# A decoder layer's feed-forward weights: block sums of 20 column tiles formed early and kept in DRAM, and another place for the last gate

## The chip, the cores and the metric

One core of a Trainium2 chip runs the kernel as one launch. The metric is the device time of an execution in microseconds (us). Engines are named as the profiler names them: PE (TensorE, matmuls), PEld (its weight loads), DVE (VectorE), ACT (ScalarE), POOL (GpSimd), SP (SyncE, which here only issues DMA transfers). A matmul's outputs go to PSUM banks; everything else lies in SBUF, in numbered slots of a tag ("three raw slots" are three buffers that tiles take in turn), or in DRAM.

## The reference

One layer of a decoder, sequence 1024, width 1024, feed-forward width 2816, all in float32:

```python
h = rms_norm(x, norm1)
z = h @ w_in                       # pool channels | q | k | v | u_s | v_s | three gates of 1024
y_a = pool_mixer(x_pool, w_pool, pool_scale) @ w_proj_a
q, k = rope(rms_norm(q)), rope(rms_norm(k))
y_b = sliding_window_attention(q, k, v, sinks) @ w_proj_b
y_c = spatial_gating(u_s, v_s, w_s, b_s, sgu_v_norm) @ w_proj_c
merged = sigmoid(g0) * y_a + sigmoid(g1) * y_b + sigmoid(g2) * y_c
x = x + merged @ w_out
h = rms_norm(x, norm2)
up = causal_dwconv(h @ w_up, conv_w, conv_b)      # width 3, over 5632 channels
gate, val = split(up, 2)
x = x + (silu(gate) * val) @ w_down
```

## The kernel before

**Arithmetic.** PE takes operands in a reduced format, so each float32 operand is split into a hi part (ACT, L86, a rounding copy) and a lo part (DVE, L87, the difference), and each product is three matmuls: hi by hi, hi by lo, lo by hi. The raw tile, loaded by SP into one of three `raw` slots, is free again when both halves of its split are done. hi and lo parts go to `w` slots (four) or, in the up stage, to `q` slots (thirteen).

**The front** (L644 to L768) works for two halves t of 512 tokens. `tok_major` forms k, v, q, u and v of the gating; then come 26 units, each a column tile of 128 of w_in: `w_gran` loads 512 KB (L276) and splits it, one unit ahead of its matmuls (L173 to L175), and `proj_ac` or `proj_b` (L625) load the matching projection. Pooling, gating and attention are generators that are spawned with a due time and stepped by `tick` when `clock`, a count of PE's microseconds, reaches it. Attention's steps are DVE's L452 to L462, then PE's flips L469. A unit adds into `part`, a tile of one slot (16 KB in each partition, which is 2 MB). When all units of a half are done, the out projection runs (w_out by L247), while, for t = 1, `norm2_flip` normalises the rows of the first half, which have lain in four `x2` slots since t = 0. The slots `x2` thus stand empty until the last unit of t = 0 fills them, and `part` is not in use in the out projection of t = 0.

**The up stage** (L776 to L960) is h @ w_up by a scheme of seven products P1 to P7 in place of eight over halves of the tokens and of the contraction. Column tile c (of 22) holds g, the gate columns (`up_raw(0, c)`), and v, the value columns (`up_raw(1, c)`), each 512 KB (L599). With a11, a12 the upper and lower halves of g and a21, a22 those of v, four sums are formed by POOL, each of 128x512: s1 = a21 + a22 (L858), s2 = s1 - a11 (L859), s3 = a11 - a21 (L860), s4 = a12 - s2 (L861). They and a11, a12, a22 are split and multiplied with ready operands of the tokens (L898 to L900, twelve matmuls a product). For tiles 0 to 6 the products P1 and P2 (PRE) run first, while the second half of the tokens is being normalised; the other five (REST) run later, between those of tiles 7 to 21 (FULL). The order of products is the list `turns`. `up_prep` of a tile begins, with its loads, LOADS = 9 turns ahead of its product and must have split it READY = 7 turns ahead. `up` then adds the PSUM result to others on ACT (L904, L910) and DVE (L916, L919, L926, L928, L939). When a tile's last product is done, `gate` gets its two results: `conv` (ACT L871, twice DVE L875) for v and g, silu on ACT (L883), the product on DVE (L884), and SP's store of 512 KB to DRAM, `gd[c]` (L885). One step of the first gate in the list follows each product. The results lie in `x` slots (four).

**The down stage** (L981 to L1163) multiplies gd with w_down by a like scheme, in two parts of 6 and 5 pairs of tiles, seven products each; `todo` lists its 77 steps of twelve matmuls (L1143 to L1145 are the three of a product). `operands` splits each step's operand three steps ahead, hi into `w`, lo into the same `x` slots. The last gate's steps are stepped here, one at each of the first eight: `if j < 8: next(gates[-1], None)`. The second part's loads are issued by `fetch` at the first step of P4 of the first part.

**What sets the order.** SP, POOL, PE and, up to the down stage, DVE and ACT get their rows from a scheduler that orders the instructions by a simulated timeline; in the down stage DVE and ACT keep the order in which the code is written.

Of the kernel before, what the change touches and what calls it, by code (L numbers as in the profile page):

```python
# [6 lines left out]
F32 = mybir.dt.float32  # L7
# [6 lines left out]
P = 128  # L14
S = 1024
# [19 lines left out]
PRE_SETS = ((0, 1), (2, 3), (4, 5, 6))  # L35
LOADS, READY = 9, 7


def trunk_kernel(tc, x, positions, norm1, w_in, q_norm, k_norm, sinks, w_pool, pool_scale,
# [104 lines left out]
    tasks = []  # L144

    def tick():
# [126 lines left out]
    def w_gran(w, c0):  # L273

        rw = raw([P, KD, P])
        sp.dma_start(rw, w[:, c0 : c0 + P].rearrange("(k p) c -> p k c", p=P))  # L276
        hi = slot("w", 4, [P, KD, P], F32R)
# [324 lines left out]
    def up_split(src, wt):  # L602
        split(wt[:, 0], wt[:, 1], src)
        return wt

    def up_early(c):
        g = up_raw(0, c)
# [31 lines left out]
    h2d = [dp.tile([P, 2, T], F32, name=f"h2d{k}") for k in range(4)]  # L639
    gd = [dp.tile([P, S], F32, name=f"gd{c}") for c in range(NC_FF)]  # L640
    mark = [None]
    spawn(setup_rest(), 24)
    st = Stream(w_in, 768, 256, KD, normed.ins)
    for t in range(2):  # L644
# [100 lines left out]
        while tasks:  # L745
            step(tasks[0])
        ss = slot("ssx", 2, [P, 32], F32)[:, 0:8]
        if t == 0:
            h = new_h()
# [87 lines left out]
    def up_prep(c, names):  # L837


        ws = wss[c, names]  # L840
        g = up_raw(0, c)
        if names == PRE:
# [4 lines left out]
            return  # L847
        v = up_raw(1, c)
        if names == REST:
# [3 lines left out]
            sp.dma_start(st["ug"][:, 0:T], pre_d[c][:, 1, :])  # L853
        a11, a12, a21, a22 = g[:, 0:HK, :], g[:, HK:, :], v[:, 0:HK, :], v[:, HK:, :]
        sa, sb = q_([P, 2, HK, P]), q_([P, 2, HK, P])
        s1, s2, s3, s4 = sa[:, 0], sa[:, 1], sb[:, 0], sb[:, 1]
        yield
        pool.tensor_tensor(s1, a21, a22, ALU.add)  # L858
        pool.tensor_tensor(s2, s1, a11, ALU.subtract)  # L859
        pool.tensor_tensor(s3, a11, a21, ALU.subtract)  # L860
        pool.tensor_tensor(s4, a12, s2, ALU.subtract)  # L861
        for n in names:
            wt = slot("w", 4, [P, 2, HK, P], F32R) if n in ("P1", "P6", "P2") else q_([P, 2, HK, P], F32R)
            ws[n] = up_split({"P1": a11, "P2": a12, "P3": s4, "P4": a22, "P5": s1, "P6": s2, "P7": s3}[n], wt)
            yield

    def conv(u, c):
# [10 lines left out]
    def gate(c, ug, uv):  # L878
        for yv in conv(uv, NC_FF + c):
            yield  # L880
        for yg in conv(ug, c):
            yield
        act.activation(yg, yg, AF.Silu)  # L883
        dve.tensor_tensor(yg, yg, yv, ALU.mult)  # L884
        sp.dma_start(gd[c], yg)  # L885
# [228 lines left out]
    for j, (part, p, q) in enumerate(todo):  # L1114
# [100 lines left out]
```

## Time and profile before

| what | value |
|---|---|
| median of 3 runs | 1316.62 us (1316.19 to 1318.61) |
| the profiled execution | 1317.56 us |
| its span in the trace | 1315.9 us, granted TensorE clock .998 of full speed |
| PE busy | 98% of the span |
| DVE, ACT, POOL busy | 74%, 46%, 14% |
| moved by DMA | 151.25 MB, 115 GB/s over the span |

The span is the time from the first to the last recorded instruction. The shares are averages over stages: the front runs to about 653 us, the up stage to about 1089 us, the down stage to the end. Which engine PE waits for differs from stage to stage and is read from the waits of each.

### The profile page before, as it was taken

Reading aid. Unit: us, or ns where it says so; the run is one execution under the profiler, and the core shown is the slowest. Engines: PE = TensorE matmul, PEld = TensorE weight load, DVE = VectorE, ACT = ScalarE, POOL = GpSimd, SP = SyncE. Lnnn points to the kernel's source line nnn. Section 1 sums busy time; section 2 is a strip of 40 time slices with the busy share of each in tenths; the row PEclk is TensorE's granted clock in tenths of the full one; section 3 lists DMA queues with packets and bytes.
Section 4 is the critical chain, followed back from the end, with each engine's and each line's share of the span. In section 5 each row is a group of like instructions: output and inputs, shape, how many; then the busy total and the mean of one; then the engine's idle time right before and its main releaser. Section 6 shows DMA issues by size and latency. Waiting matters only on the chain.

```text
span 1315.9 us, 16097 instructions
## 1 busy us (share of the span) xinstructions
PE 1283.4 (98%) x5956; PEld 1062.3 (81%) x5956; DVE 969.5 (74%) x1516; ACT 605.3 (46%) x986; POOL 190.2 (14%) x123
## 2 busy tenths in 40 slices
PE   6999999999999999999998999999999999999998
PEld 6888888888888888888877878878788787788886
DVE  6786875644578776455494889899898885986986
ACT  5555554434465555233573444434444444443432
POOL 0000000000000000000004444344542420101202
PEclk9999999999999999999999999999999999999999
DMA  6322224422432222533455223333233309418615
GB/s 235 115 85 71 80 81 126 123 72 96 161 111 74 73 78 82 158 106 104 161 207 160 86 91 113 98 108 99 65 112 112 96 32 341 107 66 287 109 20 96
DMA packets 167645, 151.25 MB, mean 115 GB/s; under 512 B 7616, under 2 KB 132494, under 8 KB 167566
## 3 DMA queue, kind: packets, MB, share of 16 engines
q1 hardware_dynamic: 163533, 142.87, 34.1%
q0 software_dynamic: 4032, 7.34, 3.8%
q8 instruction: 47, 0.77, 0.2%
q14 instruction: 33, 0.26, 0.1%
HBM read 120.30 MB, written 29.88 MB: 114 GB/s over the span
## 4 chain that ended last, share of the span: by engine, by line
PE 62%; DVE 19%; DMA 8%; ACT 5%; issue 5%; POOL 1%; SPq 0%; DVEq 0%; ACTq 0%; POOLq 0%
PE mm L173 14%; PE mm L174 14%; PE mm L175 14%; DVE x L875 7%; DMA raw<-in_w_up_dram 4%; PE bk L1144 4%; PE bk L1145 4%; PE bk L1143 4%; DVE q L87 4%; ACT x L871 2%; DMA hq<-gd 2%; DVE w L87 2%; ACT w L86 1%; PE at L445 1%; ACT x L883 1%
## 5 line engine op out<-in xcount | busy, mean ns | idle before, releaser
L173 PE MATMUL mm<-hh,w 128*128 128x512 f32 x416 | 162.6, 391 | 0.0
L175 PE MATMUL mm<-hh,w 128*128 128x512 f32 x416 | 162.5, 391 | 0.0
L174 PE MATMUL mm<-hh,w 128*128 128x512 f32 x416 | 162.4, 390 | 0.0
L858 POOL TENSOR_TENSOR q<-raw 128x512 f32<-128x512 f32 x22 | 37.1, 1685 | 844.5 <-DMA sm<-pre 652.5
L87 DVE TENSOR_TENSOR w<-raw,w 128x1024 fp32r<-128x1024 f32 (+1 forms) x96 | 93.3, 976 | 88.4 <-ACT w L86 88.4
L86 ACT ACTIVATE w<-raw 128x1024 fp32r<-128x1024 f32 (+1 forms) x96 | 82.2, 857 | 155.3 <-PE mm L174 67.0
L875 DVE SCALAR_TENSOR_TENSOR x<-q,cA,x 128x1023 f32<-128x1023 f32 x88 | 135.2, 1541 | 19.6 <-ACT x L871 19.0
L898 PE MATMUL bk<-hq,q 128*128 128x512 f32 x352 | 139.2, 395 | 6.0 <-DVE sm L916 5.1
L899 PE MATMUL bk<-hq,q 128*128 128x512 f32 x352 | 137.7, 391 | 0.0
L900 PE MATMUL bk<-hq,q 128*128 128x512 f32 x352 | 137.4, 391 | 0.0
L1144 PE MATMUL bk<-x,w 128*128 128x512 f32 x308 | 120.2, 390 | 3.0 <-DVE x L87 3.0
L1145 PE MATMUL bk<-w,x 128*128 128x512 f32 x308 | 119.9, 389 | 0.0
L1143 PE MATMUL bk<-w 128*128 128x512 f32 x308 | 94.8, 390 | 1.8 <-ACT hq L1066 1.0
L174 PEld LDWEIGHTS mm<-hh,w 128*128 128x128 f32 x416 | 78.1, 188 | 16.2
L175 PEld LDWEIGHTS mm<-hh,w 128*128 128x128 f32 x416 | 78.1, 188 | 16.0
L173 PEld LDWEIGHTS mm<-hh,w 128*128 128x128 f32 x416 | 78.1, 188 | 15.7
L87 DVE TENSOR_TENSOR wa<-raw,wa 128x512 fp32r<-128x512 f32 x72 | 49.5, 695 | 54.6 <-ACT wa L86 54.6
L898 PEld LDWEIGHTS bk<-hq,q 128*128 128x128 f32 x352 | 66.3, 188 | 25.1 <-DVE sm L916 7.6
L871 ACT ACTIVATE x<-q,cA 128x1024 f32<-128x1024 f32 x44 | 54.0, 1241 | 69.6 <-DVE q L926 36.8
L86 ACT ACTIVATE wa<-raw 128x512 fp32r<-128x512 f32 x72 | 45.1, 631 | 78.4 <-PE mm L175 67.3
L900 PEld LDWEIGHTS bk<-hq,q 128*128 128x128 f32 x352 | 66.5, 189 | 14.1
L899 PEld LDWEIGHTS bk<-hq,q 128*128 128x128 f32 x352 | 66.5, 189 | 13.4
(267 smaller groups left out, 2947.0 us busy)
## 6 DMA issues: line engine op xcount, KB each, us to landing
raw<-in_w_in_dram SPq DMA_DIRECT2D x72, 512.0 KB, 3.9
raw<-in_w_up_dram SPq DMA_DIRECT2D x51, 512.0 KB, 4.9
gd<-x SPq DMA_DIRECT2D x22, 512.0 KB, 2.8
x<-in_x_dram SPq DMA_DIRECT2D x16, 512.0 KB, 4.3
raw<-in_w_out_dram SPq DMA_DIRECT2D x16, 512.0 KB, 3.6
hq<-gd SPq DMA_DIRECT2D x28, 256.0 KB, 5.3
hq<-in_w_down_dram SPq DMA_DIRECT2D x28, 256.0 KB, 5.3
raw<-in_w_proj_b_dram SPq DMA_DIRECT2D x32, 128.0 KB, 2.8
```

The source lines that it names most:

```text
L86: split.last = act.activation(hi, src, AF.Copy).ins
L87: dve.tensor_tensor(lo, src, f(hi), ALU.subtract)
L173: pe.matmul(ps, a(0), b(0), start=first, stop=False)
L174: pe.matmul(ps, a(0), b(1), start=False, stop=False)
L175: r = pe.matmul(ps, a(1), b(0), start=False, stop=last)
L875: dve.scalar_tensor_tensor(y[:, n:], u[:, 0 : S - n], col(w), y[:, n:], ALU.mult, ALU.add)
L898: pe.matmul(ps, ws[n][:, 0, k, :], rhs[n](0, k), start=start and k == 0, stop=False, skip_group_check=True)
L899: pe.matmul(ps, ws[n][:, 0, k, :], rhs[n](1, k), start=False, stop=False, skip_group_check=True)
L900: pe.matmul(ps, ws[n][:, 1, k, :], rhs[n](0, k), start=False, stop=k == HK - 1, skip_group_check=True)
L1143: pe.matmul(ps[i], hi[:, 0, ts], hi[:, 1, :], start=start, stop=False, skip_group_check=True)
L1144: pe.matmul(ps[i], hi[:, 0, ts], lo[:, 1, :], start=False, stop=False, skip_group_check=True)
L1145: pe.matmul(ps[i], lo[:, 0, ts], hi[:, 1, :], start=False, stop=q == b - 1, skip_group_check=True)
```

## The change

The sums s1 to s4 of 20 of the 22 tiles (SUM_SETS; tiles 16 and 20 are left as they were) are formed in the front by a generator, `weight_sums`, that is stepped from `tick` like the other tasks: SP loads a tile's g and v into two scratch tiles, POOL forms the four sums in place, and POOL itself issues two stores of 512 KB to a new DRAM array, `ws`. There are three stretches: tiles 0 to 5 in the units of t = 0 from the 15th, in `x2` slots; tiles 6 to 11 in the out projection of t = 0 and the first units of t = 1, in the slot of `part`, which is allocated later for that; the last eight in the units of t = 1 from the 12th, again in `x2` slots. Since the rows of the first half then no longer stay in `x2`, they are read back from `out`, four loads of 512 KB, before the second norm. In the up stage such a tile loads only a22 of v and, for REST, nothing of g; SP loads the two pairs of sums from `ws` into `q` slots where POOL formed them before. These slots are taken READY turns ahead in place of LOADS. The last gate's two results move from `x` slots to raw slots, its steps to the down steps in GATE_STEPS, and it has one step more, ahead of the product.

```diff
+GATE_STEPS = (0, 2, 4, 12, 13, 14, 15, 16)
+SUM_SETS = (range(0, 6), range(6, 12), (12, 13, 14, 15, 17, 18, 19, 21))
+SUM_GAPS = (8.2, 8.2, 8.2)
...
     def tick():
+        while side_line and side_line[0][0] <= clock[0]:
+            side_step()
...
+    def weight_sums(cs, tiles, gap):
+        def take(c):
+            vg = tiles()
+            for o, dst in zip((1, 0), vg):
+                c0 = o * D_FF + c * P
+                with tc.issue_after(last_raw[0].ins):
+                    sp.dma_start(dst, w_up[:, c0 : c0 + P].rearrange("(k p) c -> p k c", p=P))
+            return vg
+        nxt = take(cs[0])
+        yield gap
+        for j, c in enumerate(cs):
+            v, g = nxt
+            a11, a12, a21, a22 = g[:, 0:HK], g[:, HK:], v[:, 0:HK], v[:, HK:]
+            pool.tensor_tensor(a22, a21, a22, ALU.add)
+            pool.tensor_tensor(a21, a11, a21, ALU.subtract)
+            pool.dma_start(s_d[c][:, 1], v)
+            pool.tensor_tensor(a11, a22, a11, ALU.subtract)
+            pool.tensor_tensor(a12, a12, a11, ALU.subtract)
+            pool.dma_start(s_d[c][:, 0], g)
+            yield gap / 2
+            if j + 1 < len(cs):
+                nxt = take(cs[j + 1])
+                yield gap / 2
...
-        part = slot("part", 1, [P, KD, T], F32)
...
         for i, c0 in enumerate(units):
+            if i == (14 if t == 0 else 11):
+                side_work(SUM_SETS[2 * t], own_tiles, SUM_GAPS[2 * t])
+            if i == 2:
+                side_end()
+                part = slot("part", 1, [P, KD, T], F32)
...
+                side_end()
                 x2t = [slot("x2" if t == 0 else "x", 4, [P, D], F32) for _ in range(NT)]
...
         if t == 0:
+            side_work(SUM_SETS[1], part_tiles(), SUM_GAPS[1])
+        else:
+            for b in range(NT):
+                x2[0][b] = slot("x2", 4, [P, D], F32)
+                sp.dma_start(x2[0][b], out[b * P : (b + 1) * P, :])
...
-        v = up_raw(1, c)
+        early = any(c in cs for cs in SUM_SETS)
+        if early:
+            v = raw([P, HK, P])
+            c0 = D_FF + c * P
+            sp.dma_start(v, w_up[T:, c0 : c0 + P].rearrange("(k p) c -> p k c", p=P))
...
         sa, sb = q_([P, 2, HK, P]), q_([P, 2, HK, P])
-        pool.tensor_tensor(s1, a21, a22, ALU.add)
-        pool.tensor_tensor(s2, s1, a11, ALU.subtract)
-        pool.tensor_tensor(s3, a11, a21, ALU.subtract)
-        pool.tensor_tensor(s4, a12, s2, ALU.subtract)
+        if early:
+            sp.dma_start(sa, s_d[c][:, 0].rearrange("p (j k) c -> p j k c", j=2))
+            sp.dma_start(sb, s_d[c][:, 1].rearrange("p (j k) c -> p j k c", j=2))
+        else:
...
     def conv(u, c, last):
-        y = slot("x", 4, [P, S], F32)
+        y = raw([P, S]) if last else slot("x", 4, [P, S], F32)
...
         act.activation(yg, yg, AF.Silu)
+        if last:
+            yield
         dve.tensor_tensor(yg, yg, yv, ALU.mult)
...
-        if j < 8:
+        if j in GATE_STEPS:
             next(gates[-1], None)
```

Line numbers in rows of the changed kernel are its own: L636, L637, L639, L640 are its four sums in the front, L638 and L641 their stores, L613 `up_raw`, L926 the load of a22, L938 and L939 the loads of sums, L975 the gd store, L962 and L974 conv and product of the gate, L90 the split's lo part.

POOL, before: its row of the mask, L342, in the front's start, and what stands behind it, the sums of the first tiles of the up stage in `q` slots.

```order
L342 AFFINE_SELECT sm_103_711<-sm_103_711 128x512
L858 TENSOR_TENSOR q_5989<-raw_5987 128x512
L860 TENSOR_TENSOR q_5990<-raw_5985,raw_5987 128x512
L859 TENSOR_TENSOR q_5989<-q_5989,raw_5985 128x512
L861 TENSOR_TENSOR q_5990<-raw_5985,q_5989 128x512
```

POOL in the changed kernel, from the same mask on: the first tile of the first stretch (x_296 and x_297 are its v and g in `x2` slots, ws_256 is tile 0 of `ws`).

```order
L356 AFFINE_SELECT sm_103_733<-sm_103_733 128x512
L636 TENSOR_TENSOR x_296_1972<-x_296_1972 128x512
L637 TENSOR_TENSOR x_296_1972<-x_297_1973,x_296_1972 128x512
L638 DMA ws_256<-x_296_1972 128x1024
L639 TENSOR_TENSOR x_297_1973<-x_296_1972,x_297_1973 128x512
L640 TENSOR_TENSOR x_297_1973<-x_297_1973 128x512
L641 DMA ws_256<-x_297_1973 128x1024
```

Each of 20 tiles now puts six rows there, before any row of the up stage; of the 88 sums of the up stage eight are left.

SP in the up stage, before: raw loads of g and v, what a REST tile reads back (`pre`), and a gate's store in between.

```order
L885 DMA gd_251<-x_8540 128x1024
L599 DMA raw_8450<-in_w_up_dram 128x8x128
L852 DMA sm_1317_8452<-pre_5769 128x512
L853 DMA q_8453<-pre_5769 128x512
L885 DMA gd_239<-x_8673 128x1024
L599 DMA raw_8512<-in_w_up_dram 128x8x128
L599 DMA raw_8514<-in_w_up_dram 128x8x128
```

SP in the changed kernel, at a like place (ws_259 are tile 3's sums, for REST, ws_270 those of tile 14).

```order
L975 DMA gd_245<-x_7434 128x1024
L613 DMA raw_7535<-in_w_up_dram 128x8x128
L933 DMA sm_1168_7475<-pre_5985 128x512
L934 DMA q_7476<-pre_5985 128x512
L938 DMA q_7539<-ws_259 128x1024
L939 DMA q_7540<-ws_259 128x1024
L975 DMA gd_236<-x_7579 128x1024
L926 DMA raw_7537<-in_w_up_dram 128x4x128
L938 DMA q_7599<-ws_270 128x1024
L939 DMA q_7600<-ws_270 128x1024
```

Two rows a tile, which wait for `q` slots, came into SP's queue, ahead of the gate's stores and of later raw loads.

DVE at the start of the down stage, before: splits of operands (L87), the last gate's conv (L875) in `x` slots, and sums of the down stage's own (L1020, L1021).

```order
L87 TENSOR_TENSOR x_9099<-hq_9023,w_9098 128x1024
L875 SCALAR_TENSOR_TENSOR x_9084<-q_8952,cA,x_9084 128x1023
L87 TENSOR_TENSOR x_9116<-hq_9026,w_9115 128x1024
L875 SCALAR_TENSOR_TENSOR x_9084<-q_8952,cA,x_9084 128x1022
L87 TENSOR_TENSOR x_9133<-hh_9007,w_9132 128x1024
L87 TENSOR_TENSOR x_9151<-hh_9012,w_9150 128x1024
L875 SCALAR_TENSOR_TENSOR x_9136<-q_8920,cA,x_9136 128x1023
```

DVE in the changed kernel, at the same place.

```order
L90 TENSOR_TENSOR x_9264<-hq_9188,w_9263 128x1024
L90 TENSOR_TENSOR x_9280<-hq_9191,w_9279 128x1024
L962 SCALAR_TENSOR_TENSOR raw_9249<-q_9117,cA,raw_9249 128x1023
L90 TENSOR_TENSOR x_9297<-hh_9172,w_9296 128x1024
L90 TENSOR_TENSOR x_9313<-hh_9177,w_9312 128x1024
L962 SCALAR_TENSOR_TENSOR raw_9249<-q_9117,cA,raw_9249 128x1022
L1110 TENSOR_TENSOR q_9317<-hh_9172 128x1024
```

The conv of the last gate's v stands two splits apart and in a raw slot; the conv of its g, which followed at once, comes some 20 rows later.

## Rows read from the trace of the kernel before

**Rows 1.** Page, part 1: busy us (share of the span) xinstructions.

```profile
PE 1283.4 (98%) x5956; PEld 1062.3 (81%) x5956; DVE 969.5 (74%) x1516; ACT 605.3 (46%) x986; POOL 190.2 (14%) x123
```

**Rows 2.** Stretches: us, busy of PE, PEld, DVE, ACT, POOL, PE clock, DMA share, GB/s.

```profile
693.00:726.00 33.00, 29.86 (x125) 24.16 (x125) 14.60 (x19) 11.83 (x22) 16.62 (x12) 0.95 0.53 157
726.00:1089.00 363.00, 357.62 (x1562) 291.85 (x1560) 322.36 (x334) 154.97 (x216) 146.64 (x77) 1.00 0.29 93
1188.00:1254.00 66.00, 66.00 (x293) 54.66 (x292) 48.59 (x48) 30.33 (x34) 14.12 (x16) 1.00 0.77 185
```

**Rows 3.** PE's waits, whole run: us in total, times, longest us.

```profile
PE bk L898 <- DVE sm L916: 5.1, 6, 1.5
PE bk L898 <- ACT w L86: 4.0, 2, 3.1
PE bk L1144 <- DVE x L87: 3.0, 3, 1.7
PE mm L173 <- DVE hh L91: 0.6, 1, 0.6
```

**Rows 4.** Timeline about 705: start us, us, what [idle before <-releaser].

```profile
700.15 1.29 POOL L858 TENSOR_TENSOR q<-raw 128x512 f32<-128x512 f32 x1 [652.45 <-DMA sm<-pre]
...
702.72 1.15 ACT L86 ACTIVATE q<-q 128x512 fp32r<-128x512 f32 x2 [3.37 <-POOL q L860]
...
705.44 0.50 PE L898 MATMUL bk<-hq,w 128*128 128x512 f32 x1 [3.14 <-ACT w L86]
```

**Rows 5.** Timeline about 768.

```profile
766.18 1.72 DVE L875 SCALAR_TENSOR_TENSOR x<-q,cA,x 128x1022 f32<-128x1022 f32 x1
...
768.55 0.50 PE L898 MATMUL bk<-hq,q 128*128 128x512 f32 x1 [1.15 <-DVE sm L916]
```

**Rows 6.** DVE groups while POOL is idle (1090 to 1130; 440 to 580): busy, mean ns | idle.

```profile
L875 DVE SCALAR_TENSOR_TENSOR x<-q,cA,x 128x1022 f32<-128x1022 f32 x2 | 2.6, 1278 | 0.0
...
L87 DVE TENSOR_TENSOR wp<-raw,wp 128x512 fp32r<-128x512 f32 x11 | 7.5, 686 | 0.1
```

**Rows 7.** DVE groups from 700 to 1060.

```profile
L875 DVE SCALAR_TENSOR_TENSOR x<-q,cA,x 128x1022 f32<-128x1022 f32 x38 | 64.8, 1706 | 0.4
L87 DVE TENSOR_TENSOR q<-q,q 128x512 fp32r<-128x512 f32 x62 | 63.7, 1036 | 11.0 <-ACT q L86 11.0
L875 DVE SCALAR_TENSOR_TENSOR x<-q,cA,x 128x1023 f32<-128x1023 f32 x38 | 55.5, 1459 | 17.1 <-ACT x L871 16.9
L87 DVE TENSOR_TENSOR q<-raw,q 128x512 fp32r<-128x512 f32 x21 | 26.4, 1258 | 0.0
...
L916 DVE TENSOR_TENSOR sm<-sm,bk 128x512 f32<-128x512 f32 x20 | 13.5, 676 | 0.0
```

**Rows 8.** DMA: issues (KB, us to landing); stretch 1089 to 1122; SP and ACT, 540 to 553.

```profile
raw<-in_w_up_dram SPq DMA_DIRECT2D x51, 512.0 KB, 4.9
...
out_dram<-sm POOLq DMA_DIRECT2D x16, 256.0 KB, 5.1
...
1089.00:1122.00 33.00, 30.88 (x134) 24.92 (x135) 21.61 (x20) 15.20 (x17) 0.00 (x0) 1.00 1.02 366
...
540.83 0.38 SPq L276 DMA_DIRECT2D raw<-in_w_in_dram  x1
...
552.09 1.06 ACT L86 ACTIVATE w<-raw 128x1024 fp32r<-128x1024 f32 x1 [4.58 <-PE mm L174]
```

**Rows 9.** POOL, whole run: one of its waits, and the group of L858.

```profile
POOL q L858 <- DVE x L875: 80.2, 7, 12.9
...
L858 POOL TENSOR_TENSOR q<-raw 128x512 f32<-128x512 f32 x22 | 37.1, 1685 | 844.5 <-DMA sm<-pre 652.5 <-DVE x L875 80.2 <-PE bk L900 65.7
```

**Rows 10.** Timeline of DVE at the start of the down stage.

```profile
1118.54 1.23 DVE L87 TENSOR_TENSOR x<-hq,w 128x1024 fp32r<-128x1024 f32 x1 [1.91 <-PE bk L1145]
```

**Rows 11.** Timeline of one attention block in the front, DVE and PE.

```profile
474.89 1.14 DVE L462 TENSOR_SCALAR t<-t,st 128x256 f32<-128x256 f32 x4
...
479.94 1.02 PEld L469 LDWEIGHTS at<-cA,t 128*128 128x128 f32 x8
```

More of the change, by code (lines that the diff above doesn't have):

```diff
@@ L144, in trunk_kernel, with side_step @@
     tasks = []
+    side_line = []
+    def side_step():
+        try:
+            side_line[0][0] = clock[0] + next(side_line[0][1])
+        except StopIteration:
+            side_line.pop(0)
     def tick():
+        while side_line and side_line[0][0] <= clock[0]:
+            side_step()
         again = True
@@ L275, in w_gran @@
         rw = raw([P, KD, P])
-        sp.dma_start(rw, w[:, c0 : c0 + P].rearrange("(k p) c -> p k c", p=P))
+        last_raw[0] = sp.dma_start(rw, w[:, c0 : c0 + P].rearrange("(k p) c -> p k c", p=P))
         hi = slot("w", 4, [P, KD, P], F32R)
@@ L604, in up_split, with own_tiles, part_tiles, tiles @@
         return wt
+    def weight_sums(cs, tiles, gap):
[21 more added lines that the diff above has]
+                yield gap / 2
+    def own_tiles():
+        return [slot("x2", 4, [P, KD, P], F32) for _ in range(2)]
+    def part_tiles():
+        big = slot("part", 1, [P, 4, KD, P], F32)
+        turn = [0]
+        def tiles():
+            turn[0] ^= 2
+            return big[:, turn[0]], big[:, turn[0] + 1]
+        return tiles
+    def side_work(cs, tiles, gap):
+        side_line.append([clock[0], weight_sums(cs, tiles, gap)])
+    def side_end():
+        while side_line:
+            side_step()
     def up_early(c):
@@ L640, in trunk_kernel @@
     gd = [dp.tile([P, S], F32, name=f"gd{c}") for c in range(NC_FF)]
+    s_d = [dp.tile([P, 2, KD, P], F32, name=f"ws{c}") for c in range(NC_FF)]
     mark = [None]
@@ L840, in up_prep @@
         ws = wss[c, names]
-        g = up_raw(0, c)
+        if names != REST:
+            g = up_raw(0, c)
         if names == PRE:
@@ L847, in up_prep @@
             return
-        v = up_raw(1, c)
+        early = any(c in cs for cs in SUM_SETS)
[4 more added lines that the diff above has]
+        else:
+            w2 = up_raw(1, c)
+            a21, v = w2[:, 0:HK, :], w2[:, HK:, :]
         if names == REST:
@@ L853, in up_prep, with conv @@
             sp.dma_start(st["ug"][:, 0:T], pre_d[c][:, 1, :])
-        a11, a12, a21, a22 = g[:, 0:HK, :], g[:, HK:, :], v[:, 0:HK, :], v[:, HK:, :]
+        yield
         sa, sb = q_([P, 2, HK, P]), q_([P, 2, HK, P])
-        s1, s2, s3, s4 = sa[:, 0], sa[:, 1], sb[:, 0], sb[:, 1]
-        yield
-        pool.tensor_tensor(s1, a21, a22, ALU.add)
-        pool.tensor_tensor(s2, s1, a11, ALU.subtract)
-        pool.tensor_tensor(s3, a11, a21, ALU.subtract)
-        pool.tensor_tensor(s4, a12, s2, ALU.subtract)
+        if early:
+            sp.dma_start(sa, s_d[c][:, 0].rearrange("p (j k) c -> p j k c", j=2))
+            sp.dma_start(sb, s_d[c][:, 1].rearrange("p (j k) c -> p j k c", j=2))
+        else:
+            a11, a12 = g[:, 0:HK, :], g[:, HK:, :]
+            pool.tensor_tensor(sb[:, 1], a21, v, ALU.add)
+            pool.tensor_tensor(sa[:, 0], sb[:, 1], a11, ALU.subtract)
+            pool.tensor_tensor(sb[:, 0], a11, a21, ALU.subtract)
+            pool.tensor_tensor(sa[:, 1], a12, sa[:, 0], ALU.subtract)
+        ab = {"P3": sa[:, 1], "P4": v, "P5": sb[:, 1], "P6": sa[:, 0], "P7": sb[:, 0]}
+        if names == FULL:
+            ab["P1"], ab["P2"] = g[:, 0:HK, :], g[:, HK:, :]
         for n in names:
             wt = slot("w", 4, [P, 2, HK, P], F32R) if n in ("P1", "P6", "P2") else q_([P, 2, HK, P], F32R)
-            ws[n] = up_split({"P1": a11, "P2": a12, "P3": s4, "P4": a22, "P5": s1, "P6": s2, "P7": s3}[n], wt)
+            ws[n] = up_split(ab[n], wt)
             yield
-    def conv(u, c):
+    def conv(u, c, last):
         col = lambda w: cvc[:, w * 44 + c : w * 44 + c + 1]
-        y = slot("x", 4, [P, S], F32)
+        y = raw([P, S]) if last else slot("x", 4, [P, S], F32)
         act.activation(y, u, AF.Identity, bias=col(3), scale=col(2))
@@ L878, in gate @@
     def gate(c, ug, uv):
-        for yv in conv(uv, NC_FF + c):
+        last = c + 1 == NC_FF
+        for yv in conv(uv, NC_FF + c, last):
             yield
-        for yg in conv(ug, c):
+        for yg in conv(ug, c, last):
             yield
         act.activation(yg, yg, AF.Silu)
+        if last:
+            yield
         dve.tensor_tensor(yg, yg, yv, ALU.mult)
```

1 line of the change is left out of this document (added).

## The prediction

> **What bounds the kernel now.** I read the busy times first, then busy time by stretch, then the waits of TensorE, then the rows around the longest of them. PE is busy for 1283.4 of 1315.9 us [rows 1]: nothing that adds matmuls can pay and nothing that removes other engines' work pays unless PE waits for it there. To see what PE loses I take its pitch from a stretch without a wait: 293 records begin or end in 66 us, two of them cut by the ends, so 291 matmuls of 512 columns fill it and one costs 66/291 = 0.2268 us [rows 2]. The same sum over the up stage gives two losses. From 693 to 726 us there are 123 whole matmuls, worth 27.9 us, in 33: 5.1 us are lost (A). From 726 to 1089 us there are 1560, worth 353.8, in 363: 9.2 us are lost (B) [rows 2]. The waits say where: L898 of `up` waits twice, 4.0 us, for ACT's split L86, and six times, 5.1 us, for DVE's L916; at the start of the down stage L1144 waits three times, 3.0 us, for DVE's split L87 (C). In the front PE waits for a DVE split but once, 0.6 us, after its start [rows 3]. So what can be had is A + B + C, and the front has nothing to give: it can only lose.
>
> **Whose fault A is.** PE stands 3.14 us at 705.44 for ACT's split of a hi part. ACT stood itself for 3.37 us until 702.72, for POOL's L860, and POOL had begun L858 only at 700.15 [rows 4]. The first sums of the stage come late, and PE pays. The granted clock, .95 over these 33 us [rows 2], costs 33 x .05 = 1.65 us of the 5.1.
>
> **Whose fault B is.** Ahead of the wait at 768.55, for L916, DVE runs the conv's L875 for 1.72 us from 766.18 [rows 5]. That L875 takes 1.28 us where POOL is idle [rows 6]. From 700 to 1060 us, where POOL works, the L875 of 1022 columns takes 1.706 in 38 cases, that of 1023 columns 1.459 in 38; a 512-column split of sums takes 1.036 in 62, and of raw data into the q slots 1.258 in 21 [rows 7]; the clean split of 512 takes 0.686 [rows 6]. The extra is 38 x .428 + 38 x .181 + 62 x .350 + 21 x .572 = 16.3 + 6.9 + 21.7 + 12.0 = 57 us of DVE over 88 POOL operations, .65 us each. DVE is busy 322 of the 363 us in B [rows 2], so such lumps reach PE.
>
> **The change part by part.** *Eighty POOL operations leave the up stage* (20 tiles by four). DVE gets 80 x .65 = 52 us of the 57 back there. A: P6's split then waits for a load of two sums, and no longer for four operations behind a load. The least is nothing, if the load is as late as the sums were; the most is 5.1. I take 4.5, since the load stands in SP's row as early as the raw one and lands without POOL's 2.6 us from 700.15 to 702.72. B: between nothing and 9.2. Two of 22 tiles keep their sums on POOL, and DVE's row order around L916 (L926, L875, L928, L875, L916) stays, so I let two of the six waits stand: 9.2 x 4/6 = 6.
>
> *Loads in the up stage.* A tile with ready sums reads 1 MB of sums and 256 KB less of v; a REST tile reads no g, 512 KB less. SP issues the sums seven turns ahead (READY) where the raw tiles are asked for nine ahead (LOADS). Seven turns are 7 x 12 x .2268 = 19.1 us, less 4.9 for the landing of 512 KB [rows 8]: about 14 us of cover. What stood at the slots before was POOL, at most 12.9 us at a time [rows 9], with nothing behind it but other sums. Now SP stands there, and the next raw loads and the gd store of `gate` stand behind it. I cost it at nothing because 12.9 is under 14; without that cover it is the second rival.
>
> *The last gate.* Its two results lie in raw slots, and its steps are spread to step 16 of the down stage. Before, DVE stood 1.91 us at 1118.54 for a slot of the operands' low parts [rows 10], two of whose four the gate held. C is the three waits' 3.0 [rows 3]. Most: all of it. Least: below nothing by one conv operation, 1.28 us [rows 6], if a split falls behind it at a new place. I take 2.5: two conv operations still stand between the first splits, and half a microsecond may stay. The last mult and its gd store come later too, at step 16 in place of 8. The loads that want that tile are the second part's `fetch`, at P4's first step, the 31st (five products by six pairs before it): 14 steps of 12 matmuls by .2268 are 38 us of cover for a store of 512 KB, where a load of that size lands in 4.9 [rows 8].
>
> *The front takes it all on.* POOL does 80 sums and 40 stores in three stretches; it has nothing else to do there, as its single idle time of 652.5 us shows [rows 9]. DVE pays the same 52 us there. By the longest row I have: at 474.89 DVE's L462 ends at 476.03 and the flips L469 that need it begin at 479.94, so attention has 3.9 us [rows 11], and four sums by .65 take 2.6. Loads and stores add 2.1 MB a tile, 42 MB in all, one tile in each gap of 8.2 us; a unit's own loads, 512 KB by `w_gran` and 512 KB by `proj_b`, come to 1.05. The 3.15 MB want 384 GB/s, and the most I see is 366 [rows 8]: a slip of .4 us a unit, 3 us over eight units. The tile asked for at 540.83 lands 3.9 us later and is split at 552.09, when PE frees the slot [rows 8]: 7 us of cover. SP waits there for slots too: a tile holds two of the four x2 slots for its landing, 4.9 [rows 8], its four operations, 6.7 by L858's 1.685 [rows 9], and its store, 5.1 for half the size through POOL's queue [rows 8]: 16.7 us and, for the other half, up to 5 more; the same slots are wanted again after two gaps, 16.4 us. So SP may stand some 3 us, at most 5, in `weight_sums`, with the raw loads of `proj_b` and `w_gran` behind it, under the same 7 us of cover. The reload of four residual tiles is 2 MB, 5.7 us at 366 GB/s, for the second norm, which runs beside the out projection's 192 matmuls, 43.5 us. Least loss nothing; most 8 us, if both slips, 3 and 5, came through uncovered. The nearest row is the front's own wait of .6 [rows 3]: I take two or three such, 1.5.
>
> The sum: 4.5 + 6 + 2.5 − 1.5 = 11.5 us. The profiled execution took 1317.56, so 1306.1; it lies .94 above the median of the runs, so **1305.1 us** against 1316.62. A difference under 0.2%, 2.6 us, can't be told from none.
>
> **Where a rule would part from the trace.** The rows show DVE slowed by .65 us for each POOL operation, which itself lasts 1.685 us for L858 [rows 9], and operations that read a PSUM bank not slowed (L916's mean is .676 in the same stretch) [rows 7]. The Trainium skill says, in "SBUF — State Buffer", section "SBUF: two separate sides", that VectorE and GpSimd share one port pair under an exclusive lock, held for the whole instruction, while the other fully blocks; a VectorE operation with two SBUF inputs is among those that want it. The spared PSUM reads agree with that; the price per operation here is well under a full hold. By it the up stage would not gain more than its 14.3 us in A and B, but the front would pay more, which is the third rival.
>
> **The rivals.**
> 1. *Order-bound, no change.* L916 is late because of the row it stands in, and the splits because their loads are. Then DVE's shorter operations only wait elsewhere, and A and B stay; only part of C comes, less the front's 1.5: about 2 us, 1314.6. For it: DVE's order is the same. Against: the L875 ahead of the wait was .44 us too long, and others before it. Chance .11.
> 2. *Slower: SP stands in line.* POOL's waits for slots, seven of 11.5 us in the mean and, by 65.7 over 11.5, six more [rows 9], become SP's; each ends, say, 2 us past the 14 us of cover, since the raw loads behind it start later and so the next slots come free later. 13 x 2 = 26 less the 11.5 gained: 1305.1 + 26 = 1331. It decides where SP stands more than 14 us. Against: 12.9 at the longest, and shorter when DVE is quicker. Chance .05.
> 3. *Slower or none: the front blocks.* If a POOL operation holds DVE for its whole length in the front, a tile's four take 4 x 1.685 = 6.7 us, 2.8 more than attention's 3.9. Of the 14 tiles of stretches one and three some five fall on an attention block's flips: 14 us, 1319. Against: .65 is what the rows show. Chance .04.
>
> **How the numbers follow.** My case has .80. All of A, B and C and a free front give 5.1 + 9.2 + 3.0 = 17.3 us, 1299.3; the runs lie up to 2 us apart, so 1298 is the low end. The high end, 1316, takes in the first rival; beyond it lie the other two and little else. Faster by over 0.2% (under 1314.0): .80 and a fifth of the first rival, .82; within 0.2%: the rest of it, .09, and a quarter of the third rival, .10; slower: .05 and the rest of the third, .08.
>
> **What would show it.** Right: between 700 and 1060 us the group of L875's successor with 1022 columns near 1.28 us and the split of sums near .69; L898's waits for ACT gone and those for DVE at two or fewer; no DVE idle for a slot near the start of the down stage; POOL busy some 150 us in the front, PE without waits there. Wrong: SP with waits of over 14 us for q slots and PE waiting for splits of sums; PE waits for DVE's attention operations or at the norm after the reload; or the same six waits with shorter DVE rows before them.

## The result, and the profile after

The changed kernel takes 1302.37 us (median of 4 runs, 1301.45 to 1303.43) against 1317.09 for the kernel before on the same chip: 14.7 us less, a ratio of 0.9889 with a 95% interval of 0.9874 to 0.9903. The forecast was 1305.1 with a range of 1298 to 1316. The direction and the place of each gain were right; the sizes were off by terms that partly cancel, and the mechanism of the largest gain is not settled by the experiments.

TensorE's waits in the changed kernel (us in total, times, longest us), to be held against [rows 3]:

```profile
PE at L196 <- DVE sm L597: 1.5, 1, 1.5
PE bk L988 <- ACT w L89: 1.3, 1, 1.3
PE mm L187 <- DVE part L752: 0.9, 1, 0.9
...
PE bk L988 <- DVE sm L1009: 0.8, 1, 0.8
```

L988 is the first matmul of a product (L898 before), L1009 the successor of L919, L1006 that of L916: no wait for L1006 is left, where L916 had six, and at the start of the down stage none is left either. Two waits are new, both in the front: L597 is the second norm, L752 adds a gated product into `part`.

Where the time went is read from rows that both traces have, one at each end of a piece. PE rows of the kernel before:

```profile
661.64 0.44 PE L814 MATMUL bk<-cA,x 128*128 128x128 f32 x2 [0.31 <-DVE x L803]
...
725.99 0.39 PE L898 MATMUL bk<-hq,q 128*128 128x512 f32 x1
...
1089.66 0.50 PE L898 MATMUL bk<-hq,q 128*128 128x512 f32 x1 [0.78 <-DVE sm L919]
...
1182.63 0.47 PE L1143 MATMUL bk<-w 128*128 128x512 f32 x1 [0.38 <-DVE sm L1075]
```

The same four in the changed kernel (the second is the same by the count of matmuls; the order about it differs a little):

```profile
667.30 0.44 PE L887 MATMUL bk<-cA,x 128*128 128x128 f32 x2 [0.31 <-DVE x L876]
...
725.84 0.39 PE L989 MATMUL bk<-hq,q 128*128 128x512 f32 x1
...
1080.61 0.50 PE L988 MATMUL bk<-hq,q 128*128 128x512 f32 x1 [0.78 <-DVE sm L1009]
...
1168.32 0.47 PE L1233 MATMUL bk<-w 128*128 128x512 f32 x1 [0.38 <-DVE sm L1165]
```

The front is 5.66 us longer. From there to the up stage's end it is 14.71 us shorter (from +5.66 to -9.05), and to the first exchange of banks in the down stage another 5.26 (to -14.31). The up stage splits again by the pitch of 0.2268 us [rows 2]. The stretch from 726 to 1070 us (columns as in [rows 2]), first in the kernel before:

```profile
726.00:1070.00 344.00, 338.74 (x1480) 276.55 (x1479) 308.80 (x319) 147.71 (x207) 146.64 (x77) 1.00 0.30 95
```

and in the changed kernel:

```profile
726.00:1070.00 344.00, 344.00 (x1520) 285.12 (x1519) 267.11 (x324) 155.68 (x212) 13.92 (x8) 1.00 0.39 126
```

Before, 1478 whole matmuls, 335.2 us, stood in 344: 8.8 lost here. Now 1518, 344.3 us, fill it. By the rows above the front's end to 726 us gained 5.8 (from +5.66 to -0.15), which is A, and from there to the up stage's end 8.9 (to -9.05), which is B. DVE's groups from 700 to 1060 us in the changed kernel, against [rows 7]:

```profile
L962 DVE SCALAR_TENSOR_TENSOR x<-q,cA,x 128x1022 f32<-128x1022 f32 x40 | 53.9, 1347 | 0.4
L90 DVE TENSOR_TENSOR q<-q,q 128x512 fp32r<-128x512 f32 x62 | 42.5, 687 | 14.7 <-ACT q L89 14.7
...
L90 DVE TENSOR_TENSOR q<-raw,q 128x512 fp32r<-128x512 f32 x21 | 14.4, 686 | 0.0
```

The split of sums is back from 1.036 to .687 us, the conv's second pass from 1.706 to 1.347. That DVE got its time back is plain; whether PE's waits had come of it is another question.

### The profile page after: what moved, and what is told of

The parts are those of the page before. It is cut to its first block, busy times and chain, and to the rows that moved or that the text cites. A ratio compares the mean times of both kernels' runs of the same rounds, so it can differ in the third digit from the quotient of the medians.

```text
span 1301.7 us, 16343 instructions
## 1 busy us (share of the span) xinstructions
PE 1279.5 (98%) x5956; PEld 1064.8 (82%) x5956; DVE 957.7 (74%) x1516; ACT 608.0 (47%) x986; POOL 176.8 (14%) x163
## 4 chain that ended last, share of the span: by engine, by line
PE 89%; DVE 5%; DMA 2%; ACT 2%; issue 1%; DVEq 0%; SPq 0%; ACTq 0%
PE mm L188 13%; PE mm L187 13%; PE mm L189 13%; PE bk L988 10%; PE bk L990 10%; PE bk L989 10%; PE bk L1233 5%; PE bk L1235 5%; PE bk L1234 5%; DMA raw<-in_w_up_dram 1%; PE at L459 1%; PE mm L495 1%; PE at L483 1%; DMA raw<-in_w_out_dram 1%; ACT w L89 1%
## 5 line engine op out<-in xcount | busy, mean ns | idle before, releaser
L90 DVE TENSOR_TENSOR w<-raw,w 128x1024 fp32r<-128x1024 f32 (+1 forms) x96 | 100.6, 1052 | 70.5 <-ACT w L89 70.1
L988 PE MATMUL bk<-hq,q 128*128 128x512 f32 x352 | 137.1, 390 | 0.8 <-DVE sm L1009 0.8
L962 DVE SCALAR_TENSOR_TENSOR x<-q,cA,x 128x1023 f32<-128x1023 f32 x84 | 113.2, 1353 | 20.4 <-ACT x L958 19.7
L90 DVE TENSOR_TENSOR wa<-raw,wa 128x512 fp32r<-128x512 f32 x72 | 57.2, 808 | 50.3 <-ACT wa L89 50.3
L988 PEld LDWEIGHTS bk<-hq,q 128*128 128x128 f32 x352 | 66.1, 188 | 14.9 <-DVE sm L1009 1.2
L988 PE MATMUL bk<-hh,w 128*128 128x512 f32 x176 | 69.5, 395 | 1.6 <-ACT w L89 1.3
```

What stands on the lines that cost most here:

```text
L90: dve.tensor_tensor(lo, src, f(hi), ALU.subtract)
L962: dve.scalar_tensor_tensor(y[:, n:], u[:, 0 : S - n], col(w), y[:, n:], ALU.mult, ALU.add)
L988: pe.matmul(ps, ws[n][:, 0, k, :], rhs[n](0, k), start=start and k == 0, stop=False, skip_group_check=True)
```

## The experiments

**The last gate by itself, and all but the last gate.** `gate_only` is the kernel before with `conv`, `gate` and GATE_STEPS of the change; `sums_only` is the changed kernel without them:

```diff
-        y = raw([P, S]) if last else slot("x", 4, [P, S], F32)
+        y = slot("x", 4, [P, S], F32)
...
-        if last:
-            yield
...
-        if j in GATE_STEPS:
+        if j < 8:
```

> The kernel before with the last gate's part of the change alone. If the raw slots and the later steps by themselves free the start of the down stage (my theory), its waits of L1144 for DVE's splits go and the time falls by about 5 us, to some 1312, with the six waits of the up stage for L916 as they were. If the start of the down stage was late because the up stage handed it work late (the rival), the time falls by less than 2 us, to 1315 or more, and the waits come back when the sums stay on POOL in the up stage.

Measured: 1312.29 us, ratio 0.9962 (0.9947 to 0.9977), 4.9 us less than the kernel before beside it. Its L1143's successor stands at 1176.63 where it stood at 1182.63, and 0.7 of these 6 us had been won by the up stage's end.

> The changed kernel with the last gate as before. My theory: everything of the up stage's gain stays and the down stage's 5.2 us come back, so some 1307.6, with three waits for DVE's splits at the start of the down stage. The rival, that the down stage's gain came from the quieter up stage, puts it within 1.5 us of the changed kernel, 1302 to 1304.

Measured: 1306.63 us, ratio 0.992 (0.9905 to 0.9934). TensorE's waits there have the old ones back (L1232 is L1144, L1231 is L1143):

```profile
PE bk L1232 <- DVE x L90: 3.1, 3, 1.7
...
PE bk L1231 <- ACT hq L1154: 1.0, 1, 1.0
```

Both say the same: the last gate is worth some 5 us on its own, and nothing of it hangs on the sums. It is more than the 3.0 us of DVE waits, since the wait of 1.0 for ACT's L1154 goes with them, and each wait costs about .27 us beyond its length (before, the matmuls at 1111.33, 1112.70 and 1113.04 lie 1.71 us apart in all, with a wait of .99 between, where two pitches are .45). One caution for A comes from gate_only: with an up stage as before it gains 1.1 us between 661 and 726 us too, where its wait for ACT lasted 2.0 us in place of 3.1. About 1 us of A's 5.8 may thus be no more than the difference of two traces.

**The first tile alone.** `tile7_only` has `SUM_SETS = ((7,), (), ())`, no stretch but the first, and no reading back.

> The changed kernel with the sums of tile 7 alone formed in the front; the other 21 tiles have theirs on POOL in the up stage, and nothing is read back before the second norm. Theory: the 3.1 us wait about the first tile goes (5.8 us with what follows it) and the down stage's 5.2 us stay gained, while the six waits for L916 stay: some 1306 to 1307. Rival (the first wait, too, came of slow DVE operations or of late raw loads): that wait stays and the time is 1311 to 1312.

Measured: 1311.01 us, ratio 0.9943 (0.9927 to 0.996): the rival's number, and yet not for its reason. TensorE's waits:

```profile
PE bk L990 <- DVE sm L1008: 6.9, 5, 3.0
PE bk L990 <- ACT w L89: 1.1, 1, 1.1
```

The long wait for ACT's split (3.1 us at 705) is gone: tile 7's ready sums remove it. Against gate_only, two of the six waits for L1008 (L916 before) are gone too, but a new one of 1.7 us stands at 713.85, another grew from .55 to 3.0 us, and the front ends 2.75 us later (2.2 of it in the first 50 us, of which more below); these took the gain back. So A was the late first sums, as its chain of rows [rows 4] says, and the other waits move when anything ahead of them moves.

**POOL put back beside the work.** Did slow DVE operations make the six waits? `pool_back` gives POOL four operations a tile, on the half of v just loaded and a scratch tile z; `pool_beside` has them read the sums as soon as these are loaded, next to DVE's splits of the same sums:

```diff
             sp.dma_start(sb, s_d[c][:, 1].rearrange("p (j k) c -> p j k c", j=2))
+            z = slot("z", 1, [P, HK, P], F32, ffp)
+            for i0, i1 in ((sb[:, 0], sb[:, 1]), (sa[:, 0], sb[:, 0]), (sb[:, 1], sa[:, 1]), (sa[:, 1], sa[:, 0])):
+                pool.tensor_tensor(z, i0, i1, ALU.subtract)
```

> The changed kernel with four POOL operations of 128x512 put back into the up stage for each of the 20 tiles, on the half of v just loaded and a scratch tile that nobody reads. Theory (POOL slows DVE): DVE's split of sums goes back from .69 towards 1.04 us and the conv's second pass from 1.35 towards 1.7, five or six waits for the successor of L916 return, and most of the up stage's 8.9 us after its first tiles are lost again: some 1309 to 1311. Rival (the sums were merely late as operands, or the order was better): DVE may slow but the waits stay away, 1302 to 1304.

Measured: 1303.93 us, ratio 0.9898 (0.9884 to 0.9913). None of the six waits came back, but the dose was weak: DVE's split of sums took .722 us in the mean, not 1.04, and the conv 1.507, not 1.706.

> The changed kernel with four POOL operations for each of the 20 tiles put beside the splits of its sums: they read the two tiles of sums as soon as these are loaded, two SBUF inputs each, and write a scratch tile that nobody reads; no raw slot is held by them. Theory A (DVE slowed by POOL makes the waits): the split of sums goes back towards 1.04 us, waits for the successor of L916 return, 1307 to 1311. Theory B (before, POOL's sums held the raw slots, so the next raw loads and ACT's splits came late): DVE's rows get longer, but PE hardly waits, 1302 to 1304.5.

Measured: 1303.36 us, ratio 0.9901 (0.9886 to 0.9916). Here the dose was full. The stretch from 726 to 1070 us in this kernel:

```profile
726.00:1070.00 344.00, 343.56 (x1516) 284.22 (x1515) 303.48 (x325) 154.64 (x212) 128.99 (x76) 1.00 0.38 126
```

Two of DVE's groups in that stretch:

```profile
L90 DVE TENSOR_TENSOR q<-q,q 128x512 fp32r<-128x512 f32 x59 | 47.3, 802 | 1.8 <-ACT q L89 1.8
...
L90 DVE TENSOR_TENSOR w<-raw,w 128x512 fp32r<-128x512 f32 x26 | 32.0, 1232 | 6.0 <-ACT w L89 6.0
```

In these, and in the stretch as a whole, DVE is slowed as it was before: busy 303 us, within 6 of the 309 before, in other rows than before (a split of raw data into w 1.23 us in place of .69), and PE loses half a microsecond. So DVE's share of busy time does not by itself make PE wait. DVE's rows ahead of the matmul at 922.46, which is by count the one that waited at 928.00 before:

```profile
909.08 0.69 DVE L90 TENSOR_TENSOR q<-q,q 128x512 fp32r<-128x512 f32 x1
909.68 0.68 DVE L90 TENSOR_TENSOR q<-raw,q 128x512 fp32r<-128x512 f32 x1
...
918.05 1.71 DVE L965 SCALAR_TENSOR_TENSOR x<-q,cA,x 128x1022 f32<-128x1022 f32 x1
```

The conv is as slow as before (1.72), the evacuation behind it ends 2.1 us early, and PE does not wait; at the six places together the evacuation is 1.1 to 2.5 us early, with that conv stretched at four of them. But the two splits are at their clean length at all six, where they took 1.18 and 1.78 us before. So of theory A one part falls, that DVE's load or the slow conv alone makes PE wait; what the stretch of the splits does, this run does not test.

**The raw slots, and the order of the waits.** `raw_full` loads g and v whole again for the 20 tiles, with no POOL operation; `pool_raw` adds the four sums on them, into z, while the splits still take the sums from DRAM.

```diff
-        if names != REST:
-            g = up_raw(0, c)
+        g = up_raw(0, c)
...
+        w2 = up_raw(1, c)
+        a21, v = w2[:, 0:HK, :], w2[:, HK:, :]
```

> The changed kernel with the whole raw tiles g and v loaded for each of the 20 tiles, of which the splits still read only what they need, and no POOL operation. It tells the loads from POOL's holding: theory B wants the slots held by POOL's sums, so 1302 to 1304.5 here; if the bytes and the number of raw slots taken are enough, 1306 or more with ACT waiting for raw loads.

Measured: 1301.42 us, ratio 0.9879 (0.9862 to 0.9895): no loss, so neither the bytes nor the slots of whole raw tiles were the cost.

> The changed kernel with the whole raw tiles g and v loaded again for each of the 20 tiles and the four sums formed by POOL again from them, into a scratch tile that nobody reads, while the splits still take the sums from DRAM. So POOL holds the raw slots and slows DVE as before, but no split waits for its results. Theory B, and A too: ACT waits some 3.7 us for a raw load once a tile again and the waits for the successor of L916 return, 1307 to 1312. If only the splits' own wait for the sums mattered (theory C), it stays at 1302 to 1304.5.

Measured: 1346.97 us, ratio 1.0228 (1.0209 to 1.0246), far over every expectation. Of TensorE's waits in this kernel the one that matters:

```profile
PE bk L988 <- DVE sm L1006: 24.0, 7, 4.0
```

Of SP's waits from 700 to 1090 us, the largest:

```profile
SPq L613 <- POOL z L939: 80.9, 8, 12.0
```

And of ACT's in the same time:

```profile
ACT w L89 <- DMA q<-ws: 61.0, 13, 9.2
```

SP stands up to 12 us for a raw slot that POOL's sums still read, the loads of sums stand behind it in SP's row, and ACT waits for those. It is the prediction's second rival, with another holder than the q slots. It does not repeat the kernel before, where no loads of sums stood behind; it shows what POOL's hold of a slot costs when a queue stands on it.

`pool_chain` leaves the raw slots alone and puts POOL where it was in the chain, between the sums and their splits:

```diff
+            for i0 in (sb[:, 1], sa[:, 0], sb[:, 0], sa[:, 1]):
+                pool.tensor_tensor(i0, i0, zero, ALU.add)
```

> The changed kernel with POOL put between the loads of sums and their splits: four operations of 128x512 a tile that add a tile of zeros to the sums in place, so the splits wait for POOL, in the order of the sums before; the raw slots are not touched by POOL. Theory D (before, the ring q slot, POOL's four sums, splits in ACT's and DVE's order, raw slot, next raw load was too long, and POOL's 7 us were the part that the change took out): ACT waits for raw loads again, waits for the successor of L916 return, 1306 to 1315. Theory B (it was POOL's reading of the raw slots alone that held them): DVE is slowed as in pool_beside, no wait returns, 1302 to 1304.5.

Measured: 1327.29 us, ratio 1.0087 (1.007 to 1.0104), over both expectations. The same stretch in this kernel:

```profile
726.00:1070.00 344.00, 334.30 (x1460) 272.47 (x1459) 306.31 (x313) 146.67 (x206) 134.23 (x75) 1.00 0.37 125
```

TensorE's waits in it (L1010 is L916, L1013 is L919):

```profile
PE bk L992 <- ACT sm L998: 7.6, 2, 7.3
PE bk L992 <- DVE sm L1013: 5.9, 8, 1.4
PE bk L992 <- DVE sm L1010: 4.3, 3, 1.5
```

What ACT waits for in that stretch:

```profile
ACT w L89 <- POOL q L943: 20.5, 11, 2.8
ACT q L89 <- POOL q L943: 12.9, 7, 2.2
```

DVE is as busy as in pool_beside (306 against 303 us), and eleven waits for its evacuations are there, with the first tile's wait of 7.3 us. What the edit changes between the two is that the splits wait for POOL, and with that PE waits. It is not the pattern of the kernel before: eight of the eleven waits are for L1013, of which there was one before, and ACT waits 23.8 us for raw loads, near the 19.8 of the changed kernel and not the 49.6 before, so the raw loads that the expectation named did not become late. The size overshoots too, probably since the sums are loaded first and then pass through POOL, a longer chain than before.

What stood in the kernel before is read from its rows ahead of the wait at 768.55 [rows 5]:

```profile
752.97 1.30 POOL L858 TENSOR_TENSOR q<-raw 128x512 f32<-128x512 f32 x1 [12.41 <-DVE x L875]
...
755.86 1.18 DVE L87 TENSOR_TENSOR q<-q,q 128x512 fp32r<-128x512 f32 x1
...
756.97 1.78 DVE L87 TENSOR_TENSOR q<-raw,q 128x512 fp32r<-128x512 f32 x1
...
758.28 1.61 POOL L861 TENSOR_TENSOR q<-raw,q 128x512 f32<-128x512 f32 x1
...
758.77 1.53 SPq L599 DMA_DIRECT2D raw<-in_w_up_dram  x2
...
762.58 0.63 ACT L86 ACTIVATE w<-raw 128x512 fp32r<-128x512 f32 x1 [3.71 <-DMA raw<-in_w_up_dram]
...
764.38 1.29 DVE L875 SCALAR_TENSOR_TENSOR x<-q,cA,x 128x1023 f32<-128x1023 f32 x1 [0.45 <-ACT x L871]
```

SP's waits for raw slots from 700 to 1090 us, by what ended them:

```profile
SPq L599 <- DVE q L87: 125.1, 20, 16.7
...
SPq L599 <- POOL q L861: 11.9, 7, 7.8
```

L916 stands behind the conv, the conv behind ACT's L871, and that behind a split for which ACT stood 3.7 us, until its raw load landed. SP issued the load at 758.77, when DVE's split of the raw half (756.97 to 758.75) freed the slot. DVE had run without a pause since 754.02, so it waited for none of POOL's sums there. POOL is on this path in another way: DVE's two splits run beside its four operations (752.97 to 759.89) and take 1.18 and 1.78 us where .686 is clean, and the conv of 1022 columns takes 1.72 for 1.28. That is 2.0 us on the path, more than the wait of 1.15. The same rows of the same lengths stand ahead of all six waits, of which the longest is 1.5. By these rows the two splits and the conv at their clean length would take all six waits away, if nothing else came late in their place. No run stretches these three alone, so this is read from the rows and not shown by an experiment.

**The front.** `no_front_sums` leaves out the 80 sums of the front and keeps the loads and stores, so what the up stage reads are raw halves and the block sums are missing from the computation.

> The changed kernel without the 80 POOL operations of the front; loads and stores stay, so what is stored are raw halves and the sums are left out of the computation. The front of the changed kernel loses 1.2 us at 487 (DVE's L752 late, behind DVE rows stretched by POOL), and 2.2 us about 611 to 622 (L805 and the norm's L597 late, behind SP's reload). Theory: the first goes, the second stays; if POOL's shared use of DVE's time makes both, both go; if the DMA traffic makes both, both stay.

Measured: 1297.29 us in one run beside a median of 1316.3. Neither the wait for L752 nor that for L597 is left, and the up stage begins .2 us earlier than in the kernel before. So the traffic alone makes none of the front's losses in this run; POOL's operations make both. By the rows the first comes of a slower DVE (a split of 1024 columns ahead of it takes 2.29 us, where 1.23 is clean [rows 10]), the other of a longer turn of a tile in the scratch slots. The rows of the changed kernel where the third stretch ends:

```profile
592.94 0.33 SPq L820 DMA_DIRECT2D x<-out_dram  x1
...
595.43 0.60 SPq L613 DMA_DIRECT2D raw<-in_w_up_dram  x1
...
599.11 0.33 SPq L820 DMA_DIRECT2D x<-out_dram  x1
...
603.23 0.63 ACT L89 ACTIVATE w<-raw 128x512 fp32r<-128x512 f32 x1 [7.13 <-DMA raw<-in_w_up_dram]
...
609.34 0.63 ACT L89 ACTIVATE wa<-raw 128x512 fp32r<-128x512 f32 x1 [1.28 <-DMA raw<-in_w_out_dram]
```

Of SP's waits from 300 to 640 us there:

```profile
SPq L820 <- DMA ws<-x: 10.8, 3, 7.6
```

The reload L820 stands until 592.94, and again until 599.11, for slots whose sums are still being stored. The load L613 for which ACT waits 7.1 us was issued between the two, at 595.43; after it ACT's wait of 1.3, its L805 and the norm that follows the last merge are late too.

Three variants try where the sums can go. `two17` has `SUM_SETS = (range(0, 6), (6, 7, 8, 9, 10, 11, 13, 15, 17, 19, 21), ())`, no third stretch and no reading back.

> The changed kernel without its third stretch: tiles 0 to 5 in the first, 6 to 11, 13, 15, 17, 19 and 21 in the second, the other five formed by POOL in the up stage; the rows of the first half stay in x2 and nothing is read back. If the front's losses of the third stretch (1.2 us at 487, 2 us about 611 to 622) go with it and five tiles on POOL, never two in a row, are as harmless as tiles 16 and 20 are now: some 1299 to 1300. If each tile on POOL costs its wait of about 1.5 us again, 1303 to 1306.

Measured: 1321.5 us, ratio 1.004 (1.0025 to 1.0056). The third stretch's losses went, and the longer second stretch lost 22 us where it runs into the preparation of q of the second half. Rows of DVE and POOL there:

```profile
404.81 5.45 DVE L130 TENSOR_TENSOR rs<-rq 128x16 f32<-128x16 f32 x1
...
405.25 1.31 POOL L639 TENSOR_TENSOR part<-part 128x512 f32<-128x512 f32 x1
...
406.51 1.28 POOL L636 TENSOR_TENSOR part<-part 128x512 f32<-128x512 f32 x1
...
407.74 1.26 POOL L640 TENSOR_TENSOR part<-part 128x512 f32<-128x512 f32 x1
...
408.96 1.25 POOL L637 TENSOR_TENSOR part<-part 128x512 f32<-128x512 f32 x1
...
410.71 0.17 DVE L130 TENSOR_TENSOR rs<-rq 128x16 f32<-128x16 f32 x1
```

A DVE operation of 16 columns that takes .17 us six microseconds later lasts 5.45, through four POOL operations in a row, and ends with the last of them. PE's waits in that part, 8.2 us for DVE's splits of raw tiles and 6.2 for a split of q, follow from such rows; the granted clock, .91 from 365 to 390 us and .77 from 390 to 415 (1.00 in the changed kernel), took some 8 more, by an estimate from these shares. The up stage of this kernel lost nothing with five tiles on POOL.

`twelve` has `SUM_SETS = ((7, 8, 11, 12, 15, 16), (1, 3, 5, 19, 20, 21), ())`.

> The changed kernel with sums of 12 tiles formed in the front, six in each of the first two stretches, chosen so that in the order of the up stage's turns no two neighbouring tiles have theirs formed by POOL (7, 8, 11, 12, 15, 16, 19, 20, 21 and 1, 3, 5 early). No third stretch and no reading back. If the ring through POOL needs two tiles in a row to run out of slack, as the five spaced tiles of two17 suggest, the up stage stays as in the changed kernel and the front gets back its 3.1 us of the third stretch: some 1299. If every tile on POOL costs its wait, half of the up stage's 8.9 us are lost: 1303 to 1304.

Measured: 1304.01 us, ratio 0.9891 (0.9875 to 0.9907). That is the second number, but not its reason: the front's 3 us came, and of the ten tiles on POOL only two bring a wait back (1.7 and .7 us). With a wait of .5 for ACT's L996, what PE loses as it starts again after each, and 1 us at the down stage's start, the gain is more than spent. The clock stayed at 1.00.

`short_third` has `SUM_SETS = (range(0, 6), range(6, 12), (13, 15, 17, 19, 21))`.

> The changed kernel with five tiles in the third stretch in place of eight (13, 15, 17, 19, 21); 12, 14, 16, 18 and 20 stay on POOL in the up stage, as in two17, whose up stage lost nothing. The reload of the first half's rows is asked for three gaps, 25 us, earlier. If the reload behind the stretch's end made the losses about 611 to 622, they go and the one at 487 stays: some 1300.4. If POOL's operations there slowed DVE itself, the time stays at 1302.

Measured: 1301.22 us, ratio 0.9871 (0.9853 to 0.9888). The wait for L597 is gone, the one of .9 us in the attention stays (there it ends with L476). By its profile it is better than the change by the 2.2 us of that place; by the runs the two ratios' intervals overlap, so it is at least as fast, and no more is shown.

## Why the prediction was right, and where it was not

- *The sum.* 5.8, 8.9, 5.3 and -5.7 came where 4.5, 6, 2.5 and -1.5 were taken: every gain was undersized, by 7.0 us in all, and the front's loss by 4.2. That the time came within 3 us of the forecast is in part luck.
- *What bounds the kernel.* Right: A, B and C held all that was to be had, and all of it came: 20.0 us in sum, where 17.3 was named as the most. C was undersized. The step was "C is the three waits' 3.0": ACT's wait of 1.0 at L1143 belonged to the same place, and what each wait costs beyond its length came on top (four waits, 4.0 us; 5.2 lost).
- *A.* Right in its chain (late first sums), 5.8 against 4.5 taken: the clock's loss after the wait went with it. The most of 5.1 counts from 693 us, the 5.8 from 661, and about 1 of it may be the difference of two traces.
- *B.* The gain of 8.9 lay inside 0 to 9.2, 6 taken; the two waits that were let stand for the two tiles left on POOL went too. Of "Whose fault B is" the one row that it names, the conv of 1.72 us, is not enough: pool_beside stretches it as much and PE does not wait. The step "such lumps reach PE" took DVE's share of busy time for its reason, and the share is not one: nearly the same load in pool_beside costs half a microsecond. What the rows of all six waits show in its place is a path, on which POOL stretches two splits and then the conv by 2.0 us in all. The two splits were in the prediction's sum only by their means (1.036 and 1.258 [rows 7]). pool_chain shows a second way, splits that wait for POOL, but the rows of the kernel before do not have it on the path. How much of the 8.9 came of shorter DVE rows, and how much of earlier operands and another order of loads, stays open.
- *The first rival* has "about 2 us" from C less the front's 1.5; by its own terms that is at most 1.5. It changes nothing in the range.
- *Loads in the up stage, at nothing.* Right: SP stood up to 10.9 us for a q slot, under the 14 us of cover, and no wait of PE came of it. The second rival is what pool_raw became.
- *The front.* Sized at 1.5, it cost 5.7, and the range for it (0 to 8) held that. Of this 2.3 lie before 413 us, 1.6 of it in the first 50 us. These 1.6 are not the change's: in the trace of pool_raw, whose front is the same, they are missing; its row of PE at 413.15 stands at 415.21 in the changed kernel's trace and at 412.87 before. That leaves 4.1 for POOL's operations and the reload (2.7 to 4.1 in the six other traces with this front). The stand of `weight_sums` was sized rightly (3 us, at most 5; 4.1 was the longest). The step that failed is the reload's: it was costed as a transfer of 5.7 us beside 43.5 us of matmuls, and it stood in SP's row for the scratch slots, 10.8 us in three waits and 7.6 in one, more than the 7 us of cover of the loads behind it.
- *The third rival* did not come in the changed kernel: its front lost 4.1 us, not 14 more. Its mechanism came in two17. By the Trainium skill, "SBUF — State Buffer", section "SBUF: two separate sides", a POOL operation that holds the shared port blocks a VectorE operation with two SBUF inputs altogether. The 5.45 us row of two17 agrees in that it ends with the fourth POOL operation in a row; it differs in that it is recorded as begun .44 us before the first of them, where by that section whichever starts first has the port. The prediction took a mean of .65 us as the price of one operation and set the rule aside for it; here one short operation paid over 5 us.

## What to carry to other kernels

A wait of TensorE for a late evacuation is to be followed back row by row, at each by what released it: here it led from DVE over ACT to a raw load, and from there to a split on DVE that POOL had stretched. An engine's share of busy time says little; what counts is which of its rows lie on that path. Work moved off an engine gains by what it takes out of such a path, and the busy time that it gives back elsewhere may be worth nothing. Where the work moves to has its price too: 11 tiles whose sums ran beside chains of short DVE operations with two SBUF inputs, as in normalising q, cost 22 us where six had cost under one.

## What was not expected of the hardware

A DVE operation of 128x16 lasted 5.45 us through four POOL operations in a row, and .17 without.

Executions with the same front differ by 1.7 us in their first 50 us. PE's first row starts at 9.7 us in both, and its waits are the same within .1 us; the matmuls from 19 to 21 us, first in the changed kernel, then in pool_raw:

```profile
19.00:21.00 2.00, 2.00 (x11) 2.00 (x11) 1.16 (x2) 0.00 (x0) 0.00 (x0) 1.00 0.00 0
```

```profile
19.00:21.00 2.00, 2.00 (x19) 2.00 (x18) 1.18 (x2) 0.00 (x0) 0.00 (x0) 1.00 0.00 0
```

PE does 11 matmuls in one and 19 in the other without a gap. That is what a clock still at the lower level for part of these 2 us would make; the column of the clock shows 1.00 in both, so it is argued and not shown.

The up stage of pool_raw, with PE waiting 3 to 4 us eight times, mostly some 58 us apart, ran at a mean granted clock of .94 from 726 to 1070 us where the changed kernel had 1.00, so these waits cost more than their own length.
